# Decode attention of a hybrid decoder step: cached keys turned in 32x32 blocks on VectorE, and decode run apart from prompt attention

## The chip, the cores and the metric

One core of a Trainium2 chip runs the whole program. The metric is the device time of one execution in microseconds (us); lower is better. Engines are named as in the profile: PE is TensorE's matmuls, PEld its weight loads, DVE is VectorE, ACT is ScalarE, POOL is GpSimd, SP is SyncE, whose queue issues most plain DMAs.

## The reference, cut to what matters

A two-layer decoder trunk handles one prompt of 1024 tokens and, in the same step, 8 decode sequences of 4 new tokens each with 8192 cached positions. Each layer runs three mixers on one projected input (a state-space mixer, latent attention, a gated delta rule), then one output projection and a layer norm. The change is in the latent attention of the decode tokens:

```python
s = (einsum('bthr,bsr->bhts', q_lat, kv_lat) + einsum('bthd,bsd->bhts', q_rope, k_rope)) * MLA_SCALE
s = where(k_pos <= q_pos, s, -inf)
p = softmax(s, axis=-1)
o_lat = einsum('bthr,bsr->bthr', p, kv_lat)
```

8 heads share one latent key of 256 numbers and one rotary key of 32 per position, and the latent key is also the value. A sequence has 8 heads x 4 tokens = 32 queries. The cached rows lie in pages and are fetched through a page table. All of it is in float32.

## The kernel before

Phase 1 of a layer (input projection, state-space and delta mixers, keys and queries of the prompt) ends in `mla_kv`. Phase 2 (`phase2`, L1358) holds decode attention, prompt attention, output projection and layer norm. Instructions go to TensorE in an order written out by Python generators: a `yield` marks a place where another stream may be put in. `weave_decode` (L428) takes a number from each `yield` of decode, multiplies it by SHARE = 0.6 and runs prompt attention (`mla_prompt`, L1397) until its own estimated TensorE time has used that up. `weave` (L419) does the same for prompt attention and the output projection of block 0, with SHARE2 = 1.4. The other engines' order is planned by the framework.

Decode works in 32 units a layer: 8 sequences by 4 units of 2048 cached positions. `decode_load` (L1563) issues three indirect gathers on POOL for a unit: two of latent rows (`dec_v`, 1 MB each, a partition holds 16 positions in all) and one of rotary keys (256 KB). Three units are in flight. `decode_units` (L1582) then does, for a unit:

- 32 TensorE transposes of 128x128 for the latent keys and 4 for the rotary keys, four to a PSUM bank (`ps_dT`), each bank copied to SBUF by ScalarE or VectorE (`four`, L1589);
- the scores in one PSUM bank (`ps_dS`): one product with the rotary keys against queries laid out on a block diagonal (`bd3`), then 8 products of 128 rows by 32 queries by 512 positions, one for each of two halves of the latent and four groups of positions, each group in its own 32 output partitions;
- `softmax`: the maximum of the scores (VectorE), a running maximum per sequence, the exponential with its sum (ScalarE);
- in the next unit: 4 transposes of the weights and 16 products with the values (`ps_dV`), added into the running output by VectorE with the old output rescaled.

The four groups of 32 partitions are four separate partial softmaxes; `decode_end` (L1683) combines them with the four new tokens and multiplies by the value projection. `decode_setup` (L1511) builds the absorbed queries. A float32 matmul appears in the trace as two instructions, a transpose as one.

PSUM in phase 2: prompt attention holds four banks (aS 2, aT 1, aO 1), decode four (dT 2, dS 1, dV 1). Prompt attention runs over 8 blocks of 128 queries and 4 head pairs (its `scores` and `values`), with the scores of a head in one or two banks. Output projection block 0 reads the first 384 columns of the mixers' outputs back from DRAM (`mix_load`).

Of the kernel before, what the change touches and what calls it, by code (L numbers as in the profile page):

```python
# [23 lines left out]
NT = SEQ + NS  # L24
# [9 lines left out]
SHARE2 = 1.4  # L34
SHARE = 0.6
# [93 lines left out]
class Builder:  # L129
# [298 lines left out]
    def weave_decode(self, dec, mla, rate):  # L428


        due = 0.0
        with self.tc.manual_schedule(engines={mybir.EngineType.PE}):
            for q in dec:
                due += q * rate
                while due > 0:
                    t = self.clock
                    if next(mla, self) is self:
                        break
                    due -= self.clock - t
# [918 lines left out]
    def phase2(self):  # L1358
        l = self.l
        last = l == DEPTH - 1  # L1360
        with self.pool(f"p2{l}") as p, self.psum_pool(f"p2ps{l}", aS=2, aT=1, aO=1):
            W = p.tile([128, 4672], F32, name="p2_w")
            mla = self.mla_prompt(p.tile([128, 3072], F32R, name="p2_q", tag="q", bufs=1), W)
            with self.pool(f"p2d{l}") as pd, self.psum_pool(f"p2dp{l}", dT=2, dS=1, dV=1):
                kts = self.hole.tile([128, 4096], F32, name="dec_k", tag="hole", bufs=1)
                dec = self.decode(Ring(pd.tile([128, 8496], F32, name="dec")), Ring(kts))
                self.RV = itertools.cycle([pd.tile([128, 2048], F32, name=f"dec_v{k}") for k in range(6)])
                next(mla)
                self.weave_decode(dec, mla, SHARE)
# [27 lines left out]
    def mla_prompt(self, Q, W):  # L1397
# [15 lines left out]
        def values(pr, i, heads):  # L1413
# [26 lines left out]
            self.mix_out(8 + pr, i * 128, 128, y)  # L1440

# [62 lines left out]
    def decode(self, D, RX):  # L1504

        d = {"RX": RX}
        yield from self.decode_setup(D, d)
        yield from self.decode_units(d)
        yield from self.decode_end(d)

    def decode_setup(self, D, d):  # L1511
        nc, l = self.nc, self.l
        ql, bd, cks, krs, vs, p5, st, O, m, ls, gs = (D(n) for n in (512, 1024, 64, 32, 256, 256, 64, 2048, 8, 8, 128))
        d["D"] = D.rest()
        d["load"] = self.decode_load(Ring(d["D"](1536)))
        d["ready"] = [d["load"](0, 0)]
        D = d["D"].rest()
        wkt, qs, ql_ = D(2048), D(256), D(256)
# [7 lines left out]
        q4 = ql.rearrange("p (r b q) -> p r b q", r=2, b=8)  # L1526
        yield 4.0
        for r in range(2):
            ps = self.psum("dT")
# [3 lines left out]
        bd3 = bd.rearrange("p (b q) -> p b q", b=8)  # L1533
        nc.gpsimd.memset(bd, 0.0)
        for g in range(4):
            nc.vector.tensor_copy(out=bd3[g * 32:g * 32 + 32, :, g * 32:g * 32 + 32].rearrange("p b (h t) -> p b h t", h=8),
                                  in_=qs[64:96].rearrange("p h (b t) -> p b h t", b=8))

        self.dma(cks.rearrange("p (r n) -> p r n", r=2), self.cks)
        self.dma(krs[0:32], self.krd[:, SEQ:NT])  # L1540
        ps = self.psum("dT")
# [3 lines left out]
        yield 3.0  # L1545
        ps = self.psum("dT")
        for b in range(8):
# [3 lines left out]
            self.mm(ps[0:32, w], lhsT=bd3[0:32, b, 0:32], rhs=krs[0:32], start=False, stop=True)  # L1551
        P = slice(0, 32)
        self.tt(nc.vector, p5[P], ps[P, :256], self.const[P, C_M5:C_M5 + 256], ALU.add)
        m5, l5 = st[:, 0:8], st[:, 8:16]
# [5 lines left out]
        d.update(q4=q4, bd3=bd3, vs=vs, p5=p5, m5=m5, l5=l5, O=O.rearrange("p (b r) -> p b r", b=8), m=m, ls=ls, gs=gs)  # L1560
        self.dma(d["gs"].rearrange("p (k n) -> p k n", k=4), self.gated[:, :, SEQ:NT])

    def decode_load(self, RR):  # L1563
# [9 lines left out]
        def load(b, u):  # L1573
            V, rr = [next(RV) for _ in range(2)], RR(512)
            gather(rr, rop, b * 12 + 8 + u)
            for x in range(2):
                gather(V[x], lat, b * 12 + 2 * u + x)
            return [v.rearrange("p (j r) -> p j r", j=8) for v in V], rr
# [3 lines left out]
    def decode_units(self, d):  # L1582


        nc, RX = self.nc, d["RX"]
        D = d["D"].rest()
        RP, RT, RR = Ring(D(1024)), Ring(D(32)), Ring(D(512))
        O, mcol, lcol = d["O"], d["m"], d["ls"]

        def four(out, src, copy):  # L1590
            ps = self.psum("dT")
            for m in range(4):
                self.tp(ps[:, m * 128:m * 128 + 128], src(m))
            copy(out=out, in_=ps)  # L1594
            return out

        def softmax(b, u, sc):
            t = RT(8)
            mx, nm, al, sm = t[:, 0:1], t[:, 1:2], t[:, 2:3], t[:, 3:4]
            mc, lc = mcol[:, b:b + 1], lcol[:, b:b + 1]  # L1600
            if u == 0:
                nc.vector.reduce_max(out=mc, in_=sc, axis=AX.X)
                nc.vector.tensor_scalar(out=nm, in0=mc, scalar1=-SCALE, scalar2=None, op0=ALU.mult)
            else:
                nc.vector.reduce_max(out=mx, in_=sc, axis=AX.X)
                self.tt(nc.vector, mx, mx, mc, ALU.max)
                nc.vector.tensor_scalar(out=nm, in0=mx, scalar1=-SCALE, scalar2=None, op0=ALU.mult)
                self.act(al, mc, AF.Exp, scale=SCALE, bias=nm)
                nc.vector.tensor_copy(out=mc, in_=mx)
            pe = RP(512)  # L1610
            self.act(pe, sc, AF.Exp, scale=SCALE, bias=nm, accum_out=lc if u == 0 else sm)
            if u:
                self.stt(lc, lc, al, sm, ALU.mult, ALU.add)
            return pe, al

        def weighted(V, pe, pv, ms):
            for m in ms:
                for g in range(4):
                    j = 4 * m + g
                    self.mm(pv[g * 32:g * 32 + 32, :256], lhsT=pe[:, m * 128 + g * 32:m * 128 + g * 32 + 32], rhs=V[j // 8][:, j % 8],  # L1620
                            start=m == 0, stop=m == 3)

        def total(b, u, al, pv):
            if u == 0:
                nc.vector.tensor_copy(out=O[:, b], in_=pv[:, :256])
            else:
                self.stt(O[:, b], O[:, b], al, pv[:, :256], ALU.mult, ALU.add)

        units = [(b, u) for b in range(DB) for u in range(4)]
        load, ready = d["load"], d["ready"]  # L1630
        ready += [load(0, 1), load(0, 2)]
        pend = None
        yield 2.0
        for k, (b, u) in enumerate(units):
            V, rr = ready.pop(0)
            act, dve = nc.scalar.copy, nc.vector.tensor_copy


            def keys(r, g, copy):
                return four(RX(512), lambda m: V[(4 * m + g) // 8][:, (4 * m + g) % 8, r * 128:r * 128 + 128], copy)  # L1640

            def products(r, kts):
                for g in range(4):
                    self.mm(sc[g * 32:g * 32 + 32, :], lhsT=d["q4"][:, r, b], rhs=kts[g], start=False, stop=r == 1)

            rt = four(RR(512), lambda m: rr[:, m * 128:m * 128 + 128], dve)
            k0 = [keys(0, 0, act)]
            yield 1.0
            k0.append(keys(0, 1, dve))
            yield 1.0  # L1650
            if pend:
                pb, pu, pV, pe, al = pend
                four(pe, lambda m: pe[:, m * 128:m * 128 + 128], act)
            k0.append(keys(0, 2, act))
            sc = self.psum("dS")
            self.mm(sc, lhsT=d["bd3"][:, b], rhs=rt, start=True, stop=False)
            k0.append(keys(0, 3, act))
            if pend:
                pv = self.psum("dV")
                weighted(pV, pe, pv, (0, 1))  # L1660
            k1 = [keys(1, 0, dve)]
            if pend:
                weighted(pV, pe, pv, (2, 3))
                total(pb, pu, al, pv)
                if k + 2 < len(units):
                    ready.append(load(*units[k + 2]))
            k1.append(keys(1, 1, act))
            products(0, k0)
            k1.append(keys(1, 2, act))
            yield 1.0  # L1670
            k1.append(keys(1, 3, dve))
            yield 2.0
            products(1, k1)
            pend = (b, u, V, *softmax(b, u, sc))
        yield 2.0
        pb, pu, pV, pe, al = pend
        four(pe, lambda m: pe[:, m * 128:m * 128 + 128], nc.scalar.copy)
        yield 1.0
        pv = self.psum("dV")
        weighted(pV, pe, pv, range(4))  # L1680
        total(pb, pu, al, pv)

    def decode_end(self, d):  # L1683
        nc, l = self.nc, self.l
        W = Ring(d["D"].a, d["D"].base, d["D"].size)
        wv = W(1024)
        self.dma(wv, self.i["w_uv"][l])
        P = slice(0, 32)
        Q = [slice(g * 32, g * 32 + 32) for g in range(4)]
        m, ls, m5, l5 = d["m"], d["ls"], d["m5"], d["l5"]  # L1690
# [211 lines left out]
```

## Time and profile before

| | us |
|---|---|
| median of 3 runs (lowest to highest) | 3629.96 (3621.92 to 3636.97) |
| the profiled execution: its own time / span | 3622.27 / 3620.5 |
| PE busy | 3201.3 (88%) |
| DVE busy | 2086.9 (58%) |
| ACT busy | 1394.8 (39%) |
| POOL busy | 1163.6 (32%) |
| mean granted TensorE clock | 0.949 of 2.4 GHz |
| DMA moved | 560.24 MB, mean 155 GB/s |

The span runs from the first to the last instruction of the core; the execution's own time is what the runs measure. Matmuls are pipelined and their ends are modelled, so the time from one start to the next tells more than their busy time. An idle time in square brackets is the engine's own, with what ended it.

### The profile page before, as it was taken

How to read it: one execution, taken by the hardware profiler on the slowest of the kernel's cores; microseconds unless marked ns; L12 is line 12 of the kernel's file. 1: busy time of each engine (PE TensorE's matmuls, PEld its weight loads, DVE VectorE, ACT ScalarE, POOL GpSimd, SP SyncE). 2: the span in 40 equal slices, each digit the busy share in tenths (PEclk: the TensorE clock that was granted, in tenths of full speed). 3: DMA queues.
4: the chain of work that ended last, by engine and by line, in shares of the span. 5: the costliest groups of instructions: out<-in, count | busy, mean ns of one | idle time of the engine just before them, and what ended most of it. 6: DMA issues, size and time to landing. Idle time of an engine off the chain costs nothing. (4 is left out here: it accounts for less than half of the span.)

```text
span 3620.5 us, 67281 instructions
## 1 busy us (share of the span) xinstructions
PE 3201.3 (88%) x26328; PEld 2692.3 (74%) x26328; DVE 2086.9 (58%) x4523; ACT 1394.8 (39%) x3163; POOL 1163.6 (32%) x1230
## 2 busy tenths in 40 slices
PE   6889999988779999989978999898887799998897
PEld 5888988888655655569878899888886555555797
DVE  7766355687635544446586654656865354444455
ACT  5433234333234444434433333343322344444344
POOL 4434345545421111102143443365453111111100
PEclk7999999999989999999989999998998899999898
DMA  3422324555875555444424232264577555553453
GB/s 136 122 89 89 105 65 159 177 164 185 271 227 176 188 178 175 163 150 157 153 82 128 79 102 84 66 199 158 165 234 266 183 192 184 177 174 118 160 176 133
DMA packets 313649, 560.24 MB, mean 155 GB/s; under 512 B 51292, under 2 KB 215900, under 8 KB 296308
## 3 DMA queue, kind: packets, MB, share of 16 engines
q1 hardware_dynamic: 289780, 404.94, 35.1%
q0 software_dynamic: 23552, 151.01, 12.0%
q8 instruction: 207, 3.39, 0.4%
q14 instruction: 110, 0.90, 0.1%
HBM read 426.12 MB, written 129.71 MB: 154 GB/s over the span
## 5 line engine op out<-in xcount | busy, mean ns | idle before, releaser
L181 PE MATMUL ps_pj<-xh,w_r 128*128 128x384 f32 (+1 forms) x4416 | 1214.5, 342 | 57.7 <-ACT p_cv L468 18.0
L181 PEld LDWEIGHTS ps_pj<-xh,w_r 128*128 128x128 f32 x4416 | 817.1, 196 | 79.0 <-DVE p_cv L157 20.9
L181 PE MATMUL ps_pj<-xl,w_r 128*128 128x384 f32 (+1 forms) x2208 | 734.8, 333 | 4.4 <-POOL xl L154 3.9
L181 PEld LDWEIGHTS ps_pj<-xl,w_r 128*128 128x128 f32 x2208 | 433.0, 196 | 13.3 <-POOL xl L154 10.7
L157 DVE SCALAR_TENSOR_TENSOR p_cv<-p_cv,c 128x384 f32<-128x384 f32 (+1 forms) x432 | 345.7, 803 | 80.7 <-ACT p_cv L160 67.6
L151 PEld LDWEIGHTS ps_dT<-c,dec_v 128*128 128x128 f32 x2048 | 226.9, 141 | 165.6 <-issue 99.7
L151 PE MATMUL ps_dT<-c,dec_v 128*128 128x128 f32 x2048 | 319.4, 280 | 12.1 <-ACT dec L1594 6.2
L154 POOL TENSOR_TENSOR w_r<-w_raw,w_r 128x1024 fp32r<-128x1024 f32 (+1 forms) x98 | 233.8, 2385 | 253.0 <-ACT w_r L166 208.3
L1594 ACT COPY dec_k<-ps_dT 128x512 f32<-128x512 f32 x320 | 188.1, 588 | 295.8 <-PE ps_dT L151 295.0
L181 PE MATMUL ps_m<-mix,wo_r 128*128 128x384 f32 (+1 forms) x1536 | 270.0, 335 | 16.9 <-DVE wo_r L154 15.9
L1594 DVE COPY dec_k<-ps_dT 128x512 f32<-128x512 f32 x192 | 132.2, 688 | 257.7 <-PE ps_dT L151 257.1
L181 PEld LDWEIGHTS ps_m<-mix,wo_r 128*128 128x128 f32 x1536 | 261.6, 196 | 20.7 <-DVE wo_r L154 18.5
L1571 POOL DMA_INDIRECT dec_v<-cache_kv_latent,c x128 | 122.0, 953 | 378.5 <-PE ps_dV L181 374.5
L1571 POOL DMA_INDIRECT dec<-cache_k_rope,c x64 | 61.2, 957 | 443.2 <-PE ps_dT L151 414.2
L160 ACT ACTIVATE p_cv<-p_cv 128x384 f32<-128x384 f32 x144 | 72.7, 505 | 325.2 <-DVE p_cv L157 324.2
L166 ACT CAST wo_r<-wo_raw 128x1024 fp32r<-128x1024 f32 x96 | 100.6, 1050 | 229.0 <-DMA wo_raw<-w_out 202.3
L181 PE MATMUL ps_b<-p_b 128*128 128x128 f32 (+7 forms) x1476 | 156.9, 284 | 27.0 <-ACT p_b L1011 11.7
L181 PEld LDWEIGHTS ps_b<-p_b 128*128 128x128 f32 (+5 forms) x1476 | 133.1, 160 | 44.4 <-ACT p_b L1011 13.2
L181 PE MATMUL ps_a<-p_a 128*128 128x128 f32 (+3 forms) x1108 | 142.9, 293 | 25.4 <-ACT p_a L1011 14.2
L1462 DVE TENSOR_REDUCE p_w<-ps_aS 128x1 f32<-128x512 f32 (+3 forms) x192 | 103.0, 554 | 104.2 <-PE ps_aS L181 84.4
L154 DVE TENSOR_TENSOR wo_r<-wo_raw,wo_r 128x1024 fp32r<-128x1024 f32 x80 | 101.4, 1270 | 103.2 <-PE ps_m L181 39.7
L166 ACT CAST w_r<-w_raw 128x1024 fp32r<-128x1024 f32 (+1 forms) x98 | 100.3, 1023 | 155.3 <-PE ps_pj L181 124.7
(304 smaller groups left out, 5903.8 us busy)
## 6 DMA issues: line engine op xcount, KB each, us to landing
wo_raw<-w_out SPq DMA_DIRECT2D x96, 512.0 KB, 3.6
w_raw<-w_in SPq DMA_DIRECT2D x92, 512.0 KB, 3.6
pd<-p_cv SPq DMA_DIRECT2D x164, 192.0 KB, 1.9
p_b<-pd SPq DMA_DIRECT2D x66, 256.0 KB, 2.9
p_a<-pd SPq DMA_DIRECT2D x64, 256.0 KB, 3.7
p_b<-rowd SPq DMA_DIRECT2D x48, 256.0 KB, 4.0
p_a<-rowd SPq DMA_DIRECT2D x48, 256.0 KB, 4.5
mix_raw<-mixd SPq DMA_DIRECT2D x64, 192.0 KB, 4.1
```

Of the source, the lines that this page charges most:

```text
L151: return self.nc.tensor.transpose(out, in_, self.ident[:n, :n])
L154: eng.tensor_tensor(out=out, in0=a, in1=b, op=op)
L157: self.nc.vector.scalar_tensor_tensor(out=out, in0=a, scalar=s, in1=b, op0=op0, op1=op1)
L160: self.nc.scalar.activation(out=out, in_=in_, func=func, **kw)
L166: self.nc.scalar.copy(out=hi, in_=src)
L181: return self.nc.tensor.matmul(out, lhsT=lhsT, rhs=rhs, start=start, stop=stop)
L1462: nc.vector.reduce_max(out=mx[:, b:b + 1], in_=ps[:, :w], axis=AX.X)
L1571: nc.gpsimd.indirect_dma_start(out=out, out_offset=None, in_=src, in_offset=bass.IndirectOffsetOnAxis(ap=idx[:, c:c + 1], axis=0))
L1594: copy(out=out, in_=ps)
```

## The change

Three things change together. The cached keys are no longer transposed by TensorE: VectorE turns them in blocks of 32x32 (`turn`: one instruction for 2048 columns, that is half of a unit's latents; one more of 512 for the rotary keys), from `dec_v` straight into SBUF. The keys then lie with 32 of the 256 latent numbers on 32 partitions, so the scores are summed from 9 parts (8 latent, 1 rotary) with 16 products each: 4 groups of rows by 4 groups of output partitions, 32 rows, 32 queries and 128 positions to a product. The scores take four PSUM banks, one for each group of rows; there is one such buffer. The queries are laid out for this by 256 small products at setup (`q5`). Last, decode runs before prompt attention and by itself, with the order of TensorE and VectorE written out; prompt attention then runs by itself for its first three blocks of queries, and the rest of it with output projection block 0 beside it (SHARE2 = 0.7). Up to four units are loaded ahead, in four value buffers of 2 MB.

The running maximum keeps its history per unit (`m`, `al`, `sm` have a column for each unit), so that no copy is needed; the sums are put together at the end.

```diff
-SHARE2 = 1.4
-SHARE = 0.6
+SHARE2 = 0.7
@@ phase2
+        with self.pool(f"p2d{l}") as pd, self.psum_pool(f"p2dp{l}", dS=1, dT=2, dV=2):
+            kts = self.hole.tile([128, 4096], F32, name="dec_k", tag="hole", bufs=1)
+            self.RV = itertools.cycle([pd.tile([128, 4096], F32, name=f"dec_v{k}") for k in range(4)])
+            dec = self.decode(Ring(pd.tile([128, 11880], F32, name="dec")), kts)
+            self.fixed(dec, engines=(mybir.EngineType.PE, mybir.EngineType.DVE))
         with self.pool(f"p2{l}") as p, self.psum_pool(f"p2ps{l}", aS=2, aT=1, aO=1):
             ...
-                next(mla)
-                self.weave_decode(dec, mla, SHARE)
+            self.rows = (0, 0)
+            self.fixed(mla, lambda: self.rows >= (2, 3))
@@ decode_setup (queries for parts of 32 rows)
+        for s in range(0, 8, 2):
+            ps = self.psum("dT")
+            for t in (s, s + 1):
+                for h in range(8):
+                    for g in range(4):
+                        o = (t - s) * 256 + h * 32
+                        self.mm(ps[G[g], o:o + 32], lhsT=wkt[0:64, h * 256 + t * 32:h * 256 + t * 32 + 32], rhs=qs[0:64, h], start=True, stop=True)
...
@@ decode_units
+        def turn(V, r):
+            nc.vector.transpose(T[r].rearrange("p j s k -> p j (s k)"), V[:, :, r * 128:r * 128 + 128])
+
+        def products(b, sc, parts):
+            for s in parts:
+                for i, p in enumerate(G):
+                    for g in range(4):
+                        k = rT4[p, :, g] if s == 8 else T[s // 4].rearrange("p (n g) s k -> p n g s k", g=4)[p, :, g, s % 4]
+                        self.mm(sc[G[g], i * 512:i * 512 + 128], lhsT=q5[p, s, b], rhs=k, start=s == 0, stop=s == 8)
...
+        scores = lambda: self.banks["dS"][0].tile([128, 2048], F32, name="ps_dS", tag="dS", bufs=1)
...
         for k, (b, u) in enumerate(units):
+            products(b, sc, range(4, 9))
+            more = k + 1 < len(units)
+            if more:
+                Vn, rr = ready.pop(0)
+                turn(Vn, 0)
+            pe = softmax(b, u, sc)
             if pend:
+                total(*pend)
+            if more:
+                turn(Vn, 1)
+                nc.vector.transpose(rT, rr)
+            yield
+            pt = turned(pe)
+            if more:
+                sc = scores()
+                products(units[k + 1][0], sc, range(4))
+            yield
+            pend = (b, u, weighted(V, pt))
+            if more:
+                V = Vn
+            if k + 4 < len(units):
+                ready.append(load(*units[k + 4]))
+        total(*pend)
```

`turned` is the four TensorE transposes of the weights with their copy, `weighted` the 16 products with the values, as before. `fixed` runs a generator with the order of the named engines kept, until a condition holds.

## Rows read from the trace of the kernel before

**Rows 1.** The page, busy time by engine.
```profile
PE 3201.3 (88%) x26328; PEld 2692.3 (74%) x26328; DVE 2086.9 (58%) x4523; ACT 1394.8 (39%) x3163; POOL 1163.6 (32%) x1230
```

**Rows 2.** Windows; stretch, PE, PEld, DVE, ACT, POOL busy us, clock, DMA share, GB/s.
```profile
2822.00:3460.00 638.00, 569.26 (x4635) 385.07 (x4634) 293.79 (x772) 267.02 (x619) 109.32 (x103) 0.95 0.52 170
1043.00:1675.00 632.00, 566.59 (x4634) 383.09 (x4634) 294.06 (x772) 266.81 (x619) 109.74 (x103) 0.96 0.53 173
...
1072.00:1590.00 518.00, 481.30 (x4162) 302.91 (x4164) 247.75 (x697) 231.42 (x557) 82.91 (x87) 0.99 0.49 162
```

**Rows 3.** Windows by tile: PE of ps_aS, ps_aT, ps_aO, ps_m; then p_w.
```profile
1043.00:1605.00 562.00, 74.44 (x352) 0.96 0.53 173
1043.00:1605.00 562.00, 51.39 (x288) 0.96 0.53 173
1043.00:1605.00 562.00, 50.89 (x576) 0.96 0.53 173
1605.00:1675.00 70.00, 68.97 (x384) 0.96 0.50 175
1043.00:1605.00 562.00, 101.24 (x864) 68.84 (x864) 121.53 (x383) 106.12 (x288) 0.00 (x0) 0.96 0.53 173
```

**Rows 4.** Timeline in the decode stage: start, us, engine, line, tiles, form, count.
```profile
1199.43 1.06 PE L181 MATMUL ps_dS<-dec_k,dec 128*32 128x512 f32 x8
...
1200.43 1.09 PE L151 MATMUL ps_dT<-c,dec_v 128*128 128x128 f32 x8
...
1201.28 0.71 PE L181 MATMUL ps_aS<-kT,p_q 128*128 128x512 f32 x2
...
1209.68 1.07 PE L181 MATMUL ps_dV<-dec_v,dec 128*32 128x256 f32 x16
...
1210.68 0.66 PE L151 MATMUL ps_dT<-c,dec_v 128*128 128x128 f32 x4
```

**Rows 5.** VectorE groups by form: count, busy us, mean ns, idle before.
```profile
L1605 DVE TENSOR_REDUCE dec<-ps_dS 128x1 f32<-128x512 f32 x48 | 33.2, 692 | 33.2 <-PE ps_dS L181 32.1
L157 DVE SCALAR_TENSOR_TENSOR dec<-dec,ps_dV 128x256 f32<-128x256 f32 x48 | 23.0, 480 | 15.5 <-PE ps_dV L181 15.5
...
L781 DVE STREAM_TRANSPOSE p_sb<-p_sb 128x128 f32<-128x128 f32 x32 | 9.8, 308 | 0.7
...
L1607 DVE TENSOR_SCALAR dec<-dec 128x1 f32<-128x1 f32 x48 | 7.3, 152 | 0.9
...
L1720 DVE STREAM_TRANSPOSE dec<-dec 32x256 f32<-32x256 f32 x2 | 0.8, 425 | 0.0
```

**Rows 6.** DMA: a window while gathers land; the page's line of their queue.
```profile
1301.50:1307.30 5.80, 5.07 (x42) 3.12 (x44) 2.32 (x6) 1.82 (x4) 0.94 (x1) 1.00 0.94 332
...
q0 software_dynamic: 23552, 151.01, 12.0%
```

**Rows 7.** Timeline of PE at the last decode unit of layer 0.
```profile
1562.57 1.06 PE L181 MATMUL ps_dS<-dec_k,dec 128*32 128x512 f32 x8
1566.13 0.47 PE L151 MATMUL ps_dT<-c,dec 128*128 128x128 f32 x1 [2.50 <-ACT dec L160]
```

**Rows 8.** Windows around that unit.
```profile
1562.00:1565.80 3.80, 1.63 (x12) 0.38 (x10) 3.08 (x11) 2.02 (x6) 0.00 (x0) 1.00 0.27 80
1565.80:1569.20 3.40, 3.06 (x24) 2.41 (x28) 2.55 (x14) 1.17 (x5) 0.00 (x0) 0.50 0.94 303
1569.20:1573.00 3.80, 3.80 (x43) 2.27 (x43) 3.46 (x19) 0.00 (x0) 0.00 (x0) 1.00 0.72 222
```

**Rows 9.** Tile ps_dT: duration ns min/median/max, first and last start.
```profile
L151 PE MATMUL ps_dT<-c,dec_v x2048: 272/273/421, 1088.7 to 3340.7; 128*128 128x128 f32 x187
```

**Rows 10.** Timeline: the sum of the queries' two parts.
```profile
1067.95 0.42 DVE L154 TENSOR_TENSOR dec<-dec 96x256 f32<-96x256 f32 x1 [16.97 <-DMA p_q<-qd]
```

**Rows 11.** Timeline of PE in the delta mixer: sixteen products in diagonal blocks.
```profile
299.82 0.45 PE L181 MATMUL ps_a<-p_sa 32*32 32x32 f32 x32
300.20 0.44 PE L181 MATMUL ps_pj<-xh,w_r 128*128 128x384 f32 x1
```

More of the change, by code (lines that the diff above doesn't have):

```diff
@@ L426, in weave, with fixed @@
                 due, t = due - (self.clock - t), self.clock
[L428 to L439, printed above, removed]
+    def fixed(self, gen, until=lambda: False, engines=(mybir.EngineType.PE,)):
+        with self.tc.manual_schedule(engines=set(engines)):
+            for _ in gen:
+                if until():
+                    break
     def store(self, k, nb, src):
@@ L1502, in mla_prompt, with decode @@
         yield from pend
-    def decode(self, D, RX):
-        d = {"RX": RX}
+    def decode(self, D, kts):
+        d = {"T": [kts[:, r * 2048:r * 2048 + 2048].rearrange("p (j s k) -> p j s k", j=16, s=4) for r in range(2)]}
         yield from self.decode_setup(D, d)
@@ L1532, in decode_setup @@
             nc.scalar.copy(out=q4[:, r].rearrange("p b (h t) -> p b h t", h=8), in_=ps[:, :256].rearrange("p (h b t) -> p b h t", h=8, b=8))
[L1533 to L1541, printed above, removed]
+        ps = self.psum("dV")
         for r in range(2):
@@ L1573, in load @@
         def load(b, u):
-            V, rr = [next(RV) for _ in range(2)], RR(512)
+            V, rr = next(RV), RR(512)
+            for x in range(2):
+                gather(V[:, x * 2048:x * 2048 + 2048], lat, b * 12 + 2 * u + x)
             gather(rr, rop, b * 12 + 8 + u)
-            for x in range(2):
-                gather(V[x], lat, b * 12 + 2 * u + x)
-            return [v.rearrange("p (j r) -> p j r", j=8) for v in V], rr
+            return V.rearrange("p (j r) -> p j r", j=16), rr
@@ L1580, in decode_load @@
         return load
     def decode_units(self, d):
-        nc, RX = self.nc, d["RX"]
+        nc, G, T, q5, O = self.nc, d["G"], d["T"], d["q5"], d["O"]
         D = d["D"].rest()
[L1587 to L1595, printed above, removed]
+        RP, RT, rT = Ring(D(1024)), Ring(D(1024)), D(512)
@@ L1610, in softmax @@
-            pe = RP(512)
-            self.act(pe, sc, AF.Exp, scale=SCALE, bias=nm, accum_out=lc if u == 0 else sm)
-            if u:
[L1613 to L1617, printed above, removed]
+                nc.vector.tensor_scalar(out=nm, in0=mx, scalar1=-SCALE, scalar2=None, op0=ALU.mult)
+            else:
+                old = d["m"][:, b, u - 1:u]
+                nc.vector.tensor_scalar(out=nm, in0=mx, scalar1=-SCALE, scalar2=old, op0=ALU.mult, op1=ALU.min)
@@ new lines, in softmax, with turned @@
+            self.act(pe.rearrange("p (n i k) -> p i n k", n=4, i=4), s4.rearrange("p i (n k) -> p i n k", n=4), AF.Exp,
+                     scale=SCALE, bias=nm, accum_out=d["sm"][:, b, u:u + 1])
+            if u:
+                self.act(mx, old, AF.Exp, scale=-1.0, bias=nm)
+            return pe
+        def turned(pe):
+            ps, pt = self.psum("dT"), RT(512)
+            for n in range(4):
+                self.tp(ps[:, n * 128:n * 128 + 128], pe[:, n * 128:n * 128 + 128])
+            nc.scalar.copy(out=pt, in_=ps)
+            return pt
@@ L1618, in weighted @@
+        def weighted(V, pt):
+            pv = self.psum("dV")
+            for n in range(4):
                 for g in range(4):
[L1619 to L1623, printed above, removed]
+                    self.mm(pv[G[g], :256], lhsT=pt[:, n * 128 + g * 32:n * 128 + g * 32 + 32], rhs=V[:, 4 * n + g], start=n == 0, stop=n == 3)
+            return pv
@@ L1624, in total @@
+        def total(b, u, pv):
             if u == 0:
@@ L1632, in decode_units @@
+        turn(V, 1)
+        nc.vector.transpose(rT, rr)
+        self.decode_new(d)
+        sc = scores()
+        products(0, sc, range(4))
         pend = None
-        yield 2.0
         for k, (b, u) in enumerate(units):
[L1635 to L1650, printed above, removed]
-            if pend:
[L1652 to L1674, printed above, removed]
@@ L1685, in decode_end @@
         W = Ring(d["D"].a, d["D"].base, d["D"].size)
-        wv = W(1024)
-        self.dma(wv, self.i["w_uv"][l])
+        wv = d["wv"]
         P = slice(0, 32)
         Q = [slice(g * 32, g * 32 + 32) for g in range(4)]
-        m, ls, m5, l5 = d["m"], d["ls"], d["m5"], d["l5"]
+        m5, l5 = d["m5"], d["l5"]
+        nm, ls = W(8), W(8)
+        nc.vector.tensor_copy(out=nm, in_=d["m"][:, :, 3])
+        nc.vector.tensor_copy(out=ls, in_=d["sm"][:, :, 0])
+        for u in range(1, 4):
+            self.tt(nc.vector, ls, ls, d["al"][:, :, u])
+            self.tt(nc.vector, ls, ls, d["sm"][:, :, u], ALU.add)
         mg = W(32)
```

91 lines of the change are left out of this document (47 added, 44 removed).

## The prediction, made before the changed kernel was run

> **What bounds the kernel now.** I read the busy shares first: TensorE is busy 88% of the span, no other engine over 58% [rows 1], so I looked for the stretches that the change touches and for what fills TensorE in them. The windows show one stretch per layer, from the first prompt score to the first output product of block 1 (the end of block 0): 1043 to 1675, which is 632 us, and 2822 to 3460, which is 638 us [rows 2]. Inside it TensorE is busy 481 of 518 us while decode and prompt attention run woven; VectorE is at 248, ScalarE at 231, the DMA engines at 0.49 and the granted clock at 0.99 [rows 2]. The reader is to see that TensorE alone is full there, and that it works off two things.
>
> By tile, prompt attention holds it 74 + 51 + 51 = 177 us and output block 0 another 69 us [rows 3]; the rest is decode, 32 units a layer. So prompt attention is already finished within the decode stretch, and output block 0 runs alone behind it. That is the order the change turns round.
>
> **What goes, what comes.** A unit now has 40 transposes (eight take 0.85 us to the next product [rows 4]), so 4 us and more, with eight key products of 512 columns at about 0.25 us each, the rope product, and 16 weighted products. The transposes of keys (32) and rope (4) go, with their nine copies out of PSUM on ScalarE and VectorE. What comes is set by four candidates for the time *c* of one unit.
>
> VectorE: two turns of 2048 columns and one of 512. No row shows one so long. The row of 128 columns takes 0.308 us, the row of 256 takes 0.425 [rows 5], so 0.117 more for 128 columns: 0.31 + 15 x 0.117 = 2.07 us for 2048, 0.66 for 512. The other end would be 16 times the short row, 4.9 us. I take 2.1, since the two rows already differ by length alone. With the maximum at 0.69, the scaling at 0.15 and the weighted total at 0.48 [rows 5] this is 4.2 + 0.66 + 1.32 = 6.2 us, 6.5 with the gaps between six instructions.
>
> DMA: a unit gathers 2 MB of latents and 0.25 MB of rope, 2.36 million bytes. While two gathers filled the DMA engines to 0.94 they moved 332 GB/s; the page has 151.01 MB in 12.0% of sixteen engines, so 347 GB/s [rows 6]. That gives 6.8 to 7.1 us a unit. Gathers now run four units ahead, so latency is hidden, not the rate. Before, a unit lasted 518 / 32 = 16 us and DMA was half idle.
>
> TensorE's own work: 144 products of 32 rows and 128 columns. Four products of 512 columns, one in each column block, take 1.00 us to the next start, and eight of 256 columns also 1.00 [rows 4], so a block needs 0.25 us for 128 columns of this type. If all sixteen 32 x 32 blocks work at once, 144 / 16 x 0.25 = 2.25 us; if only four do, 9.0 us. The stretch before shows four column blocks at once, and 32 instructions on four diagonal blocks start within 0.38 us [rows 11]; sixteen it does not show. I take 2.25, because row blocks and column blocks each overlap there. With four transposes (0.44) and 16 weighted products (2.0) that is 4.7 us, where it was about 9.3.
>
> The uncovered chain: sc is one buffer of four banks, so between the last product of a unit and the transposes of its weights TensorE has nothing to do: the maximum, the scaling, the exponential. Before, prompt attention filled this, except at the last unit. There the products start at 1562.57, run 1.06 us, and the transposes wait until 1566.13, 2.50 us idle [rows 7]. Some of that was ScalarE finishing prompt exponentials, so I take 2.2. A unit on this chain takes 4.7 + 2.2 = 6.9 us at full clock.
>
> So at full clock VectorE (6.5), DMA (7.0) and TensorE's chain (6.9) are nearly equal, and c is about 7.0. But the same place shows what the hole does. TensorE was busy 1.63 of 3.8 us, and then its granted clock stood at 0.50, the 1.2 GHz level, from 1565.8 to 1569.2 although it was busy 3.06 of these 3.4 us; then it was 1.00 again [rows 8]. Each unit of the new stage has such a hole. 3.4 us at half speed put off 1.7 us of work. If each unit pays that, c = 8.6; I take most units, 8.3. Ends for c: 6.5 from below, 13.7 from above (four blocks at once: 2.2 + 0.44 + 9.0 + 2.0).
>
> POOL issues three gathers a unit, under 4 us of 8; the code that keeps the running maximum loses two small instructions. Both lie beside the chain and count nothing; were POOL to wait for a value buffer, the three units loaded ahead cover it.
>
> **The sum for one layer.** Ahead of the first unit: TensorE's first key transpose came at 1088.7 [rows 9], 45 us in, since the queries arrived only at 1068 behind three units' gathers [rows 10]. In this stage four units are asked for at once, and SP's small loads of queries, new keys, gates and w_uv queue beside them, so they are no earlier; the turns of unit 0 wait on VectorE behind the query sum. The queries are built as 256 small products instead of 16, but run at four blocks. I keep 42 us (33 to 55). Units: 32 x 8.3 = 266. Behind the last unit: its weights and total, about 5 us, and the end of decode, a chain of some fifty short VectorE instructions, then three steps on TensorE, which now nothing hides: 15 us; together 20.
>
> Then prompt attention, 177 us of TensorE, with the 69 us of output block 0 woven into its later part: 246 if TensorE is never idle, and nearly so because the output products fill its waits. VectorE has 122 and ScalarE 106 for prompt attention there [rows 3], far from the end. From below 215, if the busy rows hold pipeline tails that overlap; from above 290, if the 45 us in which TensorE stood idle in the stretch before (632 less 567 busy [rows 2], less what waited for the queries) all stay with prompt attention.
>
> 42 + 266 + 20 + 246 = 574 us, against 632 and 638: 58 and 64 saved, 122 in all. The profiled execution took 3622.3 us (span 3620.5) and becomes 3500; the median of the runs shown is 3630, 8 above it, so I forecast 3508. The break-even is c = 10.2.
>
> On the sixteen blocks the Trainium skill ("TensorE: Matmul & The Clock Gate", Measured speedup vs the span model) gives 10.6-fold for sixteen tiles of 32 x 32, where I count 16. By that the products take an estimated 3.4 us instead of 2.25, and the time would be about 3581. No run here shows sixteen yet; the overlap of four is full in rows 4.
>
> **Rivals.**
> (a) The clock stays at 2.4 GHz: the hole is shorter than at 1566, since no foreign exponentials stand in the way. Then DMA sets 7.0 a unit: 532 a layer, 3424. For it: three limits that close leave TensorE busy two thirds of the time. Against it: rows 8.
> (b) The sixteen blocks overlap only in part, as if ten worked: 144 / 10 x 0.25 = 3.6 us, c = 9.65, 617 a layer, 3594. For it: nothing here shows more than four at once. Against it: rows 11 run blocks that differ in rows and columns both.
> (c) Prompt attention alone does not keep TensorE full, 290 us: 3596. For it: its scores wait for two PSUM banks. Against it: output block 0 stands between its steps.
> (d) On the other side: the low level holds through the whole decode stage. The 4.7 us of work become 9.4, with the hole 11.6 a unit, 679 a layer: 3718, slower. Place: the hole in each unit; it decides from c = 10.2, that is when a unit loses 3.3 us against its 6.9. For it: rows 8, and 32 holes in a row. Against it: at 1569 the clock was back after one such stretch of full work.
> (e) Also slower: only four blocks work at once, so the change does not do what it says. c = 13.7, 746 a layer, 3852. Against it: the interleaved starts of rows 4 and 11.
>
> **Chances.** Forecast 0.40, own range 3450 to 3570; (a) 0.18; (b) 0.10; (c) 0.10; (d) 0.10; (e) 0.12. The range 3400 to 3720 holds all but (e) and a few hundredths below, where prompt attention takes only 215. About half a per cent, 18 us, is what a measurement can tell. Faster: 0.38 + 0.18 + 0.08 + 0.07 = 0.71; the same: 0.02 + 0.02 + 0.03 + 0.01 = 0.08; slower: 0.21.
>
> **What would show it.** Right: a decode stage of 290 to 350 us a layer with nothing of prompt attention in it; turns of 2.1 us; the products of a unit in 2 to 3 us; DMA near 0.8 busy and 280 GB/s; a hole of about 2 us on TensorE in each unit and a granted clock of 0.7 to 0.9; then some 250 us of prompt attention with output block 0 inside it. Wrong: turns of 4 us and more (VectorE sets the unit at 12), products of 8 us (e), a clock of 0.5 throughout (d), or an output block 0 that still stands alone behind prompt attention.

## The result, and the profile after

The changed kernel takes 3928.8 us (median of four runs, 3925.2 to 3938.5) against 3632.7 before: ratio 1.082, 95% interval 1.079 to 1.086. The forecast was 3508, its range ended at 3720. The profiled execution took 3925.2 us, 303 more than the profiled one of before.

The page of the changed kernel first: busy times, the granted clock in forty slices, and the queues of the gathers and of the instruction code.

```profile
PE 3310.1 (84%) x42328; PEld 2764.2 (70%) x42328; DVE 2234.7 (57%) x4325; ACT 1228.1 (31%) x2859; POOL 1161.2 (30%) x1236
...
PEclk8999999999867666799989999999987767658998
...
q0 software_dynamic: 23552, 151.01, 10.8%
q8 instruction: 332, 5.44, 0.6%
```

TensorE is busy for less of a longer span than in [rows 1], the clock is at 5 to 7 tenths in two stretches, one per layer, and the code queue brings 332 packets of 16 KB. Before, it brought 207:

```profile
q8 instruction: 207, 3.39, 0.4%
```

These packets are TensorE's code: the trace has 85,129 records of TensorE (weight loads, products and its sequencer's own) and had 53,087, in both kernels 256 to a packet. The windows (decode, prompt attention with output block 0, and 220 us from the middle of decode; products and weight loads with their counts, granted clock, DMA share, GB/s) answer to [rows 2]:

```profile
core 0: us, PE busy (x) PEld busy (x) DVE busy (x) ACT busy (x) POOL busy (x), PEclk, DMA share, GB/s
1043.00:1560.00 517.00, 379.71 (x11056) 230.80 (x11054) 217.98 (x252) 59.83 (x149) 92.67 (x108) 0.68 0.44 152
1560.00:1820.00 260.00, 234.20 (x1555) 183.52 (x1556) 147.36 (x413) 121.59 (x311) 19.02 (x8) 0.91 0.36 103
1120.00:1340.00 220.00, 170.77 (x5224) 101.97 (x5207) 102.22 (x96) 24.01 (x60) 44.58 (x49) 0.71 0.50 175
```

Decode and then the rest last 777 us where the forecast had 574. Prompt attention is nearly as forecast (260 for 246). Decode is not: the first key product starts at 1094.9, the last weighted one at 1524.5, so 32 units take 430 us, 13.4 each on the average and 13.8 as the median step of both layers; the forecast was 8.3. One unit on TensorE (start, length, operation, count; in brackets the idle time before and its releaser):

```profile
1300.15 3.64 PE L180 MATMUL ps_dV<-dec_v,dec 128*32 128x256 f32 x32
1303.72 1.38 PE L180 MATMUL ps_dS<-dec_k,dec 32*32 32x128 f32 x47
1305.35 1.26 PE L180 MATMUL ps_dS<-dec_k,dec 32*32 32x128 f32 x75 [0.25 <-issue]
...
1309.06 1.11 PE L150 MATMUL ps_dT<-c,dec 128*128 128x128 f32 x4 [1.92 <-ACT dec L159]
1310.10 4.15 PE L180 MATMUL ps_dS<-dec_k,dec 32*32 32x128 f32 x128
1314.19 3.64 PE L180 MATMUL ps_dV<-dec_v,dec 128*32 128x256 f32 x32
```

The hole is there (1.92 us idle), the weighted products take 3.6 us, the four transposes 1.1, and the 144 products (288 instructions, two passes each) 7.2 us instead of 2.25. VectorE's turn is as forecast:

```profile
L1606 DVE STREAM_TRANSPOSE dec_k<-dec_v x128: 2265/2306/2314, 1067.2 to 3439.2; 128x2048 f32<-128x2048 f32 x128
```

### The profile page after: what moved, and what is told of

Same layout as the page of the kernel before. It is cut to its first block, busy times and chain, and to the rows that moved or that the text cites. A ratio compares the mean times of both kernels' runs of the same rounds, so it can differ in the third digit from the quotient of the medians.

```text
span 3923.4 us, 99032 instructions
## 1 busy us (share of the span) xinstructions
PE 3310.1 (84%) x42328; PEld 2764.2 (70%) x42328; DVE 2234.7 (57%) x4325; ACT 1228.1 (31%) x2859; POOL 1161.2 (30%) x1236
## 5 line engine op out<-in xcount | busy, mean ns | idle before, releaser
L180 PE MATMUL ps_dS<-dec_k,dec 32*32 32x128 f32 x16384 | 386.4, 346 | 55.8 <-issue 52.5
L180 PEld LDWEIGHTS ps_dS<-dec_k,dec 32*32 32x32 f32 x16384 | 258.6, 120 | 194.6 <-issue 170.1
L1606 DVE STREAM_TRANSPOSE dec_k<-dec_v 128x2048 f32<-128x2048 f32 x128 | 295.1, 2307 | 157.0 <-PE ps_dS L180 157.0
L180 PE MATMUL ps_m<-mix,wo_r 128*128 128x384 f32 (+1 forms) x1536 | 320.3, 350 | 29.7 <-DVE wo_r L153 18.0
L159 ACT ACTIVATE dec<-ps_dS,dec 128x512 f32<-128x512 f32 x64 | 44.0, 687 | 701.8 <-DVE dec L1624 533.3
L180 PE MATMUL ps_dV<-dec_v,dec 128*32 128x256 f32 x2048 | 215.0, 588 | 1.5 <-ACT dec L1636 1.5
L1618 DVE TENSOR_REDUCE dec<-ps_dS 128x1 f32<-128x512 f32 x64 | 44.2, 691 | 292.9 <-PE ps_dS L180 292.9
L153 POOL TENSOR_TENSOR wo_r<-wo_raw,wo_r 128x1024 fp32r<-128x1024 f32 x16 | 38.2, 2389 | 451.1 <-PE ps_m L180 217.1
L150 PE MATMUL ps_dT<-c,dec 128*128 128x128 f32 x264 | 59.2, 363 | 124.3 <-ACT dec L159 122.6
L180 PE MATMUL ps_a<-p_a 128*128 128x128 f32 (+3 forms) x1108 | 141.6, 291 | 25.4 <-ACT p_a L1004 14.2
```

The lines of the kernel that those rows point to most:

```text
L150: return self.nc.tensor.transpose(out, in_, self.ident[:n, :n])
L153: eng.tensor_tensor(out=out, in0=a, in1=b, op=op)
L159: self.nc.scalar.activation(out=out, in_=in_, func=func, **kw)
L180: return self.nc.tensor.matmul(out, lhsT=lhsT, rhs=rhs, start=start, stop=stop)
L1606: nc.vector.transpose(T[r].rearrange("p j s k -> p j (s k)"), V[:, :, r * 128:r * 128 + 128])
L1618: nc.vector.tensor_reduce(out=mx, in_=s4, axis=AX.XY, op=ALU.max)
```

## Experiments

The table has for each kernel the TensorE instructions of one unit (a load and a product for each pass; the texts on record below count them higher, 656 for 648, 400 for 392 and 270 for 180), the median step from unit to unit (which instruction one steps by moves it by up to 0.4; the mean of lag_big8 is 8.5), TensorE instructions per us and clock in 1120:1340, and the time (one execution each, but four of after and of lag and five of before_free; before: 3628 to 3643 beside them).

| kernel | instr. a unit | us a unit | instr. per us | clock | us |
|---|---|---|---|---|---|
| after | 648 | 13.8 | 47 | 0.71 | 3928.8 |
| fill16 | 680 | 13.3 | 51 | 0.91 | 3897.4 |
| lag | 648 | 14.1 | 47 | 0.74 | 3931.5 |
| narrow | 648 | 13.0 | 49 | 0.59 | 3886.4 |
| wide | 648 | 13.8 | 47 | 0.90 | 3922.2 |
| lag_merge | 648 | 14.2 | 45 | 0.77 | 3934.5 |
| direct | 648 | 12.7 | 50 | 0.74 | 3855.5 |
| lag_direct | 648 | 13.4 | 48 | 0.77 | 3870.5 |
| nogather | 648 | 10.2 | 63 | 0.83 | 3726.2 |
| lag_nogather | 648 | 9.7 | 63 | 0.85 | 3698.8 |
| lag_big8 | 392 | 7.9 | 45 | 0.95 | 3611.1 |
| big8_pad | 648 | 14.9 | 43 | 0.82 | 3979.9 |
| before_apart | 180 | 12.0 | 15 | 1.00 | 3765.6 |
| before_free | 180 | 12.5 | 16 | 1.00 | 3599.8 |

**First theory: the hole lowers the clock (fill16, lag).** fill16 puts spare work into the hole, lag real work.

```diff
 # fill16, ahead of pt = turned(pe)
+            ps = self.psum("dT")
+            for n in range(16):
+                self.tp(ps[:, n % 4 * 128:n % 4 * 128 + 128], self.ident)
 # lag: weighted() of unit k - 1 between softmax(k) and turned(k)
-            pend = (b, u, weighted(V, pt))
+            pend = (b, u, V, pt)
```

> Sixteen spare 128x128 transposes of the identity matrix stand on TensorE in the hole of each unit, between its last product and the transposes of its weights; nothing else changes. Theory A (the hole lowers the clock): with the hole filled the granted clock of the decode stage goes from 0.68 to above 0.95; then products take 3.9 us (nine rounds of 0.435 us, as in the stretch at 1.00 from 1305.3 to 1307.0 of the changed kernel), the weighted products 2.0, four transposes 0.44, the hole still 2.1, 0.4 in between: 8.9 us a unit instead of 14.0, so 3925 - 64 x 5.1 = 3600 us. Rival B (the 32x32 blocks themselves keep the clock low, hole or not): the clock stays at 0.5 to 0.75, sixteen transposes last 3.4 us at the low level and stick out of the hole by 1.3, 15 us a unit, 3925 + 64 x 1 to 1.3 = 3990 to 4010 us.

> The weighted products of a unit come one unit later, into the hole in which TensorE waits for the next unit's exponentials; the load of the unit four ahead becomes three ahead. All work is there. Theory A (the hole lowers the clock): about 2.0 of 2.1 us are filled with real work, the clock goes above 0.95, TensorE needs 3.9 + 0.44 + 2.0 + 0.4 = 6.8 us a unit, VectorE 2 x 2.31 + 0.67 + 1.32 = 6.6, DMA 7.0: 7.2 us a unit instead of 14.0, 3925 - 64 x 6.8 = 3490 us, which is below the kernel before (3630) as well. Rival B (small blocks keep the clock low whatever stands in the hole): the unit loses only the hole of 2.1 us, 12 us, 3925 - 64 x 2.1 = 3790 us, still above before.

fill16 got the clock and not the time; lag, timed in three rounds, is level with the changed kernel (1.081 of before, 1.078 to 1.084). Windows of fill16, then of lag:

```profile
1120.00:1340.00 220.00, 183.92 (x5655) 124.19 (x5654) 107.33 (x99) 25.27 (x64) 47.70 (x51) 0.91 0.51 180
```

```profile
1120.00:1340.00 220.00, 162.88 (x5139) 99.11 (x5127) 100.40 (x96) 24.04 (x60) 45.29 (x48) 0.74 0.49 171
```

The theory falls as the first cause: with the hole filled, 5139 products pass in 220 us of lag where 5224 did, and in fill16, at a clock of 0.91, some 5390 besides the spare ones. The timeline of lag shows what came instead:

```profile
1306.70 0.66 PE L150 MATMUL ps_dT<-c,dec 128*128 128x128 f32 x4
1307.29 0.89 PE L180 MATMUL ps_dS<-dec_k,dec 32*32 32x128 f32 x43
1308.38 0.43 PE L180 MATMUL ps_dS<-dec_k,dec 32*32 32x128 f32 x6 [0.20 <-issue]
1309.11 0.43 PE L180 MATMUL ps_dS<-dec_k,dec 32*32 32x128 f32 x6 [0.30 <-issue]
1309.84 3.48 PE L180 MATMUL ps_dS<-dec_k,dec 32*32 32x128 f32 x162 [0.30 <-issue]
1316.03 0.74 PE L180 MATMUL ps_dS<-dec_k,dec 32*32 32x128 f32 x37 [2.71 <-issue]
```

The waits of 1120:1340 say how much of it there is (us in total, times, longest), in lag and then in the changed kernel:

```profile
PE ps_dS L180 <- issue: 56.6, 58, 4.6
```

```profile
PE ps_dT L150 <- ACT dec L159: 30.6, 16, 2.0
PE ps_dS L180 <- issue: 17.6, 30, 2.8
```

In a wait for "issue" TensorE waits for nothing that a semaphore shows. Its long stops stand at a fixed place of the code: from 1300 to 1400 lag has eight of over 1.2 us from start to start with products on both sides, and counting all of TensorE's records from the first, its sequencer's among them, all eight fall at number 192 modulo 256. 256 records are one 16 KB packet of the code queue (the texts below call it a page), and TensorE goes on 1.2 to 1.6 us after such a packet has landed: one landed at 1314.78, products went on at 1316.03.

**What limits the products themselves (narrow, wide).**

```diff
-  self.mm(sc[G[g], i * 512:i * 512 + 128], lhsT=q5[p, s, b], rhs=k, start=s == 0, stop=s == 8)
 # narrow
+  w = 128 if s == 0 else 64
+  self.mm(sc[G[g], i * 512:i * 512 + w], lhsT=q5[p, s, b], rhs=k if s == 0 else k[:, 0:2], start=s == 0, stop=s == 8)
 # wide
+  k = rT[p, 0:256] if s == 8 else T[s // 4][p, 8 * (g % 2):8 * (g % 2) + 8, s % 4]
+  self.mm(sc[G[g], i * 512:i * 512 + 256], lhsT=q5[p, s, b], rhs=k, start=s == 0, stop=s == 8)
```

> Each of the 128 key and rope products behind the first sixteen of a unit takes 64 columns of keys instead of 128: half of the scores leave out all but the first 32 numbers of the latent. Same number of instructions. Theory W (in each 32x32 block the weights of a pass are loaded between the passes, not behind them): a round of sixteen products now lasts 0.435 us at full clock, 2 x (0.107 stream + 0.11 load); with 64 columns 2 x (0.053 + 0.11) = 0.33. Eight of nine rounds lose 0.105, at the mix of clocks of this stage some 1.3 us a unit: 3925 - 64 x 1.3 = 3840. Rival I (the instructions are let in at a fixed pace, 32 loads and 32 products in 0.435 us): a round stays at 0.435 and the time at 3925. Rival S (the stream alone counts): eight rounds halve, 3 us a unit, 3730. If the lower load of TensorE costs still more clock, the rounds tell all the same.

> Each of the 144 key and rope products of a unit takes 256 columns of keys instead of 128, the other half being keys of neighbouring groups: scores are not the reference's. Same number of instructions. Theory W: a round at full clock goes from 0.435 to 2 x (0.213 + 0.11) = 0.65 us, 9 x 0.215 = 1.9 us a unit at full clock, 3 us at the mix of this stage: 3925 + 64 x 3 = 4120. Rival I (fixed pace of 0.435 us for 32 instructions, which covers a stream of 0.427): the round stays near 0.44 and the time at 3925 to 3960. If the fuller columns lift the clock, as B would have it, the time falls instead and the granted clock of the stage shows it.

The time hardly moved either way (13.0 and 13.8 us a unit). The rounds did: from the starts of 32 products one behind the other at clock 1.00, the median is 0.31 us with 64 columns, 0.42 with 128 and 0.62 with 256. 64 columns more add about 0.11 each time, and what is left at no columns is 0.20 us, as W has it for the round. I and S are out for the round. W's reason, loads not hidden in a block, does not hold in general: in lag_big8 below eight products of 256 columns take 0.43, the stream alone.

In time W missed: it had 3840 for narrow and 4120 for wide, and wide came out next to where I had it (3925), for another reason. The window of wide, then its wait for issue there:

```profile
1120.00:1340.00 220.00, 185.36 (x5198) 105.09 (x5192) 102.63 (x97) 24.01 (x60) 45.32 (x49) 0.90 0.49 175
```

```profile
PE ps_dS L180 <- issue: 1.0, 2, 0.7
```

The longer products of wide fill the time in which the changed kernel waited (1.0 us of issue for 17.6), and the clock goes to 0.90 although the hole stays. Wide is limited by its own work, not by a wait for code.

**Second theory: TensorE's code comes too slowly beside the gathers (lag_nogather, nogather, lag_big8).**

```diff
 # nogather, lag_nogather
+            if b == 0:
+                for x in range(2):
+                    gather(V[:, x * 2048:x * 2048 + 2048], lat, b * 12 + 2 * u + x)
+                gather(rr, rop, b * 12 + 8 + u)
 # lag_big8: for s > 0 two column blocks with 256 columns each (their line is left out here)
-                    for g in range(4):
+                    for g in range(4 if s == 0 else 2):
```

> As lag (weighted products in the hole), and only the four units of the first sequence are gathered; the 28 later units of a layer turn, score and weigh what lies in the value buffers, so their cache is left out. In lag TensorE stood still 1.2 to 5.3 us at a time, each time at the same place of its code modulo 256 instructions, and the code fetch that ended the stop began 2.8 to 4.6 us behind the last such place while gathers ran, 1.1 to 1.3 us behind it otherwise. A unit is 656 TensorE instructions, 2.56 such pages, at 5.3 us a page 13.6 us. Theory F (code pages wait behind gathers): without gathers a page takes about 3.5 us, 2.56 x 3.5 = 9.0 us a unit: 3930 - 64 x 4.7 = 3630 us. Rival P (the pace of code is 5.3 us a page whatever the gathers do): 13.6 a unit, 3915 to 3930 us. Rival G (no code limit at all, gathers themselves held the unit back): VectorE sets 6.8 us a unit, 3490 us.

> The changed kernel with its hole, and without the gathers of the 28 later units of a layer, whose cache is so left out. Theory A+F (two limits lie close together: the low clock that the hole brings, 13.8 us a unit, and the code, 13.3 to 13.6): taking the gathers away frees the code alone, the hole stays and the clock with it; only the stops at page ends go, about 0.4 us a unit: 3925 - 64 x 0.4 = 3900 us, granted clock 0.65 to 0.72 in the decode stage. Rival F alone (code is what held the changed kernel too, the clock only followed): 9 to 10 us a unit, 3640 to 3690 us, with a clock above 0.85.

> As lag, but from the second sixteenth of the contraction on the key and rope products run on eight 32x32 blocks with 256 columns each instead of sixteen with 128: the same number of columns goes through TensorE, in 80 products a unit instead of 144 (the scores are not the reference's: the upper 64 rows hold the first products alone). A unit has 400 TensorE instructions instead of 656. Theory F: 1.56 pages at 5.3 us are 8.3 us; TensorE itself needs 0.435 + 8 x 0.65 + 2.0 + 0.44 + 0.4 = 8.5 us at full clock, so 9 us a unit: 3930 - 64 x 4.7 = 3630 us. Rival (TensorE's own work is what a unit lasts): half of the blocks, longer products; the unit grows to 15 us or more, 4010 us and above.

nogather is the decisive one. Hole and products are as in the changed kernel, and a unit falls from 13.8 to 10.2 us, 200 us in all: the clock rose from 0.71 to 0.83 although the hole stayed. So the hole alone does not set the clock, and my "A+F" (3900) falls; "F alone" is the nearer one, but it had 3640 to 3690 and a clock above 0.85, measured 3726 and 0.83. The windows of nogather and its share of the code queue, and that queue in the same window of the changed kernel:

```profile
1120.00:1340.00 220.00, 176.04 (x6949) 118.14 (x6944) 137.73 (x129) 31.88 (x80) 0.00 (x0) 0.83 0.02 4
...
q8 instruction: 54, 0.88, 1.6%
```

```profile
q8 instruction: 41, 0.67, 1.3%
```

54 packets in 220 us are one in 4.1 us, 41 one in 5.4. In lag_nogather, without hole and gathers, TensorE still stops at the ends of code pages (42.3 us of issue in these 220), so 63 instructions per us is the most that this code reached in that window. lag_big8 keeps the gathers and takes 40% of the instructions away:

```profile
1120.00:1340.00 220.00, 185.65 (x4952) 120.80 (x4936) 161.33 (x154) 38.37 (x96) 69.61 (x74) 0.95 0.75 276
```

A unit takes 7.9 us (8.5 on the average), the DMA engines move 276 GB/s, and the instructions per us are close to those of the changed kernel, 45 for 47.

**The converse (big8_pad).**

```diff
+  self.mm(sc[G[2 + g], i * 512 + 256:i * 512 + 264], lhsT=q5[p, s, b], rhs=T[0][p, g, s % 4, 0:8], start=True, stop=True)
```

> As lag_big8, and beside each of the 64 products of 256 columns of a unit stands a spare one of 8 columns, on one of the eight blocks that lag_big8 leaves idle; nothing reads it. A unit has 656 TensorE instructions again, as in lag, but the work of lag_big8. Theory F (a unit lasts as long as its code pages take beside the gathers): 2.56 pages at 5.3 us, 13.6 us a unit instead of 7.85: 3611 + 64 x 5.75 = 3980 us, and long stops of TensorE at a fixed place modulo 256 instructions. Rival (work, not code): 256 more starts at 6.8 ns are 1.7 us a unit at most, 3611 + 64 x 1.7 = 3720 us.

3979.9, as theory F has it: the instructions are back, and a unit takes 14.9 us. The spare products are not free: at clock 1.00 a round takes 0.61 us with them and 0.43 without, which is 1.5 us for the eight rounds of a unit, 2.9 if all ran at the low level. The time grew by 5.8 us a unit, so the rival's account (1.7 at most) is too small. In the window 1300 to 1400 all seven stops of over 1.2 us inside the products are at 192 modulo 256, as in lag.

```profile
1120.00:1340.00 220.00, 161.74 (x4783) 97.39 (x4773) 91.42 (x88) 21.87 (x55) 40.89 (x45) 0.82 0.43 158
```

The twelve kernels with small products have 473 such stops in all: every one stands at 192 modulo 256, and at every one TensorE goes on 1.2 to 1.6 us after a code packet has landed.

**What in the gathers does it (lag_merge, direct, lag_direct).**

```diff
-  gather(V[:, x * 2048:x * 2048 + 2048], lat, b * 12 + 2 * u + x)
 # lag_merge, for both x at once
+  gather(V, lat, b * 12 + 8 + u)
 # direct, lag_direct
+  self.dma(V[:, x * 2048:x * 2048 + 2048], lat[o:o + 128])
```

> As lag, with the two gathers of a unit's latents made one (one row of 16 KB for each partition instead of two of 8 KB): 2 gather instructions a unit instead of 3, the same bytes. All work is there. TensorE's short stops of 0.67 us among the products all stood beside GpSimd's gather instructions. If these stops come from the instruction itself: 2 instead of 3 parts, some 0.4 us a unit, and the page waits stay, as they go with the bytes: 13.4 us a unit, 3905 us. If the page waits too go with the number of gathers or of their pieces: 11.5 to 12 us a unit, 3790 to 3820 us. If neither: 3930 us.

> The changed kernel, with the latents and rope keys of each unit fetched by three plain loads of SyncE's queue instead of GpSimd's gathers: the same bytes into the same buffers, from the front of the cache, so the page table is left out. Theory T (code waits behind the traffic): as the changed kernel, 13.8 us a unit, 3925 us. Rival G (code waits behind the gather instructions or their pieces): as without any gathers, 10.2 us a unit, 3726 us, and no short stops of 0.67 us among the products.

> As direct, with the weighted products in the hole. Theory T: 14.0 us a unit, 3930 us. Rival G: 9.7 us a unit, as in lag_nogather, 3699 us.

One gather less changed nothing. Plain loads of the same bytes gave 73 of the 203 us that leaving the gathers out gave, and 61 of 233 with the hole filled (lag_direct). So both count: most of it is the traffic, a quarter to a third the gathers' form. The short stops (0.5 to 0.76 us between two loads inside the products, 1110 to 1420) are the gathers' own: 46 in the changed kernel, all beside a gather instruction of GpSimd, 2 in direct, 4 in nogather. They do not go with the number of gathers: 60 in lag, 57 in lag_merge.

**The other half of the change alone (before_alone, before_apart, before_free).** Keys turned by TensorE as before, decode first.

```diff
-                next(mla)
-                self.weave_decode(dec, mla, SHARE)
+                with self.tc.manual_schedule(engines={mybir.EngineType.PE}):
+                    for _ in dec:
+                        pass
+            self.rows = (0, 0)
+            with self.tc.manual_schedule(engines={mybir.EngineType.PE}):
+                for _ in mla:
+                    if self.rows >= (2, 3):
+                        break
```

> The kernel before with the other half of the change alone: keys are still turned by TensorE, 40 transposes a unit, but decode runs by itself, and prompt attention follows with output block 0 inside it, as in the changed kernel. TensorE has (481 - 177) / 32 = 9.5 us of decode a unit, in some 270 instructions, 1.05 code pages. Theory F (the loss of the changed kernel is the code of the small products): 1.05 pages at 5.3 us are hidden, a unit takes 10 to 11 us, a layer 42 + 340 + 20 + 260 = 662 against 635: 3632 + 54 = 3690 us. Rival O (it is the order: decode without prompt attention lets the clock fall): at the low level for three quarters of the stage the unit takes 14 to 16, 3630 + 64 x 4 to 6 = 3890 to 4010 us.

> What before_alone was to be: keys turned by TensorE, prompt attention strictly behind decode, since its buffers now lie where decode's lay (in before_alone the planner drew prompt attention's products in between the units). TensorE has 9.5 us of decode a unit, about one code page. Theory F (the loss of the changed kernel is the code of the small products): 10.5 to 12 us a unit, a layer 42 + 352 + 20 + 260 = 674 against 635, 3634 + 78 = 3710 us, with no stop of TensorE at page ends. Rival O (it is the order: decode without prompt attention beside it lets the clock fall to the low level for most of the stage): 14 to 16 us a unit, 3890 to 4010 us.

before_alone (3613.2) did not do what it was meant for: its prompt products start at 1074.9, between the units, since nothing held them back and the planner put them there. before_apart, with the prompt buffers allocated only once decode's are free, does it: 12.0 us a unit at a clock of 1.00 and 3765.6 us. Rival O falls (the order does not bring the clock down), and so does my 3710: TensorE is idle 16 of 220 us and a unit takes the upper end.

```profile
1120.00:1340.00 220.00, 204.16 (x1650) 109.83 (x1649) 76.66 (x168) 78.13 (x159) 51.75 (x55) 1.00 0.58 200
```

Against 3629.7 before, 136 us of the loss are the order, and the other 163 to 3928.8 what the changed kernel has beyond it, VectorE's turn with its small products above all; that half was not run without the order. before_alone timed again as before_free:

> The same kernel as before_alone, timed: decode's products in their own fixed order, prompt attention's in theirs, and the planner puts the one between the other, instead of the rate of 0.6 by which the kernel before weaves them; output block 0 goes into the end of prompt attention. In the one look TensorE was busy 99 to 100 of 100 us through the stage at a granted clock of 1.00, a unit with its share of prompt attention took 12.4 us and the time was 3613. Theory W (the finer weave fills what the fixed rate left empty): 3613 us, 0.994 of before. Rival: one look of a kernel that scatters by 8 us to either side; 3634, no difference.

3599.8 us, 0.992 of before (0.991 to 0.994, five rounds): the version that beats both. It differs from before in two things, the finer weave and the place of output block 0, which were not taken apart. TensorE has next to no idle time left in decode:

```profile
1120.00:1340.00 220.00, 219.44 (x1810) 126.72 (x1808) 96.73 (x252) 92.28 (x215) 49.86 (x53) 1.00 0.62 208
```

## Why the prediction was wrong

**The step that failed** is "What comes is set by four candidates for the time *c* of one unit". There was a fifth: the supply of TensorE's instructions. The change replaces 180 instructions a unit by 648, and 648 in the 8.3 us of the forecast are 78 per us. The fastest 50 us of before have 26; the kernels here with such products ran 43 to 51 beside the gathers, and 63 without them. 648 at 47 are 13.8 us, which is the measured unit told in another way; that the supply is the cause is shown by nogather, lag_big8 and big8_pad from three sides, and by the place of the stops. The page of before had the code queue, with 207 packets; I read its rate nowhere.

**The products** ("I take 2.25") were mis-sized as well: 9 x 0.417 = 3.75 us at full clock, so 16 x 0.25 / 0.417 = 9.6 blocks' worth, which is rival (b), and not (e). That alone would have given c = 9.8 and some 3603 (rival (b), with 3.6 us, has 3594). The Trainium skill ("TensorE: Matmul & The Clock Gate", Measured speedup vs the span model) has 10.6-fold; the trace, at 9.6, is close to it, and I should have taken it rather than 16.

**The clock.** Rival (d) looks right (0.71, and a time above 3718), but its mechanism is not the cause: with the hole kept and the gathers gone the clock is 0.83 and a unit takes 10.2 us, with the hole kept and longer products (wide) it is 0.90; with the hole filled and the gathers kept it is 0.91, and a unit takes 13.3. The stops for code lower the clock as the hole does. In lag TensorE stands still for 5.2 us, and right behind that the granted clock is 0.50 although it is busy all the time; in the 3 us behind each of lag's 62 stops it is 0.56 on the average, where the window has 0.74:

```profile
1367.80:1373.00 5.20, 0.27 (x13) 0.00 (x0) 1.71 (x1) 0.00 (x0) 0.00 (x0) 0.85 0.46 178
1373.00:1376.40 3.40, 3.40 (x105) 2.16 (x109) 1.21 (x3) 0.25 (x1) 0.00 (x0) 0.50 0.02 5
```

My reading is that the low clock then hides part of the wait for code: 17.6 us of issue in 220 in the changed kernel, 56.6 in lag. How the 13.8 us divide between waits for code, short stops and the low clock that they bring, no run takes apart.

**What held.** The turn (2.31 for 2.07), the hole (1.9 to 2.2 for 2.2), prompt attention with block 0 (260 for 246), and VectorE and DMA are no bound (half busy). Setup to the first key product is 52 us instead of 42, the end 35 instead of 20, 6.5 of it a wait for the queries' load. Units are +164 of the +203 us of a layer.

**The break-even** was put at c = 10.2; nogather has c = 10.2 and is 83 us above before. The setup, end and prompt terms, 39 us a layer too low, are the difference.

## What to carry over

Before many small products take the place of a few large ones, count the instructions of the engine and divide by the time forecast: a rate that no stretch of the trace has yet reached can be a cost of its own, and the code queue on the page is where it shows. Idle time without a releaser that always stands at the same instruction number modulo one packet is its sign. A low clock next to idle time is a symptom until the idle time has been removed: fill it, and see whether the time falls. And test the two halves of a change apart: here the order half alone lost 136 us, the rest lost 163 more on top of it, and the order half, left to the planner and with output block 0 moved, gained 30.

## What the runs showed of the hardware

- TensorE's code comes in 16 KB packets, 256 instructions (85,129 records in 332). In units of 648 instructions TensorE ran 63 per us without gathers (nogather), and 47 beside 175 GB/s of them; stops of up to 5.7 us (lag) stand at one place modulo 256.
- Sixteen 32x32 blocks do run at once, but each round of sixteen two-pass products carries about 0.20 us beside the stream (0.31, 0.42, 0.62 us for 64, 128, 256 columns). Eight blocks with 256 columns carry none (0.43), and eight spare products of 8 columns beside them bring it back (0.61).
- GpSimd's gather instructions bring stops of some 0.67 us to TensorE's small products, which plain loads of the same bytes do not.
- Open: why a code packet comes later beside traffic. Its transfer takes the same 1.0 us with and without gathers, so it is its start that is late; and the pace does not simply go with the traffic (39 packets in 220 us at 171 GB/s in lag, and 39 at 276 GB/s in lag_big8, which waits less for them).
- Open too: what the short stops are, and where the 0.20 us come from. A version with all the work and half of the instructions was not built: eight blocks leave the scores on half of the partitions.
